# A hybrid encoder on one core: another order for the first transfers, and a warming product between two transposes

## The chip, the core and the metric

The kernel runs on one core of a Trainium2 chip. Its engines are TensorE (PE, matrix products and transposes; its loads of the stationary operand are listed as PEld), VectorE (DVE), ScalarE (ACT), GpSimd (POOL) and SyncE (SP). Each executes its own instructions in order and waits for the others by semaphores. DMA transfers between the chip's memory and the core's working memory are issued by SP, ScalarE and GpSimd, each on a queue of its own, and are carried out by 16 DMA engines. The metric is the device time of one execution in microseconds, as the median of several.

## What is computed

The reference is an encoder of two layers on 256 tokens of 1024 channels, in float32:

```python
def reference(x, w_in, w_pool, ...):
    h = x
    for layer in range(DEPTH):          # 2
        h = h + _token_mixer(_rmsnorm(h, norm1[layer]), w_in[layer], ...)
        h = h + _conv_ffn(_rmsnorm(h, norm2[layer]), w_up[layer], ...)
    return _rmsnorm(h, norm_f)

def _rmsnorm(x, g):
    y = x * lax.rsqrt(jnp.mean(x * x, axis=-1, keepdims=True) + EPS)
    return y * g
```

The token mixer multiplies the normalised x (256 x 1024) by w_in (1024 columns of pooling, 3 x 1536 of queries, keys and values, 2048 of gates), mixes tokens by means over windows and by attention in three groups of heads, and projects back. The second sub-layer is a gated MLP with 2816 channels and a convolution over three tokens. For this document only the very beginning matters: the first norm of x, and the first columns of values, `rmsnorm(x, norm1[0]) @ w_in[0][:, 4096:5120]`.

## The kernel before

All products are made at float32's accuracy out of three products of split operands: a number is kept as a rounded high part and the rest as a low part, and high x high, low x high and high x low are added up in PSUM. For every piece of weights ScalarE rounds the high part and VectorE subtracts the rest (`Weights.open_next`); TensorE then multiplies. Weights come through three raw buffers, which SP loads as soon as a buffer is free.

The beginning is `values_of_x`, written out by hand: its instructions stand on each engine in the order of the program, with no scheduler in between. It makes the first 1024 columns of values for all 256 tokens before x has been normalised. The norm's row norm1[0] scales the rows of the weights, so it must stand as a column, one number for each channel: `gcol`. The norm's other factor, one number per token, comes later, when the sums are copied out. So these are the steps:

- `begin` issues the first transfers. x is held as h with even tokens (t = 0) and odd tokens (t = 1) apart; it comes in parts of 256, 256 and 512 channels for each t (`part_of_x`, L342). The first two megabytes of weights come as `loads[0]` and `loads[1]` in four transfers of 256 KB each (`load_by`, L142), the columns 0 to 511 and 512 to 1023 of the first 512 rows. The norm's row comes as 8 rows of 128 numbers, `rows8`, whose tile is named grows (L349).
- TensorE makes five products of a tile of ones, whose result nobody uses (`warm`, L377, `WARM[0]` = 5, tile gain_ps), transposes rows8 into PSUM (L369), and VectorE copies it to gcol (L370).
- `turn_x` (L719) transposes blocks of x, 128 x 128, into PSUM (xt_ps), since TensorE needs channels on the partitions; ScalarE or VectorE rounds them to xuh (L726), and VectorE leaves the rest in xul (L723). The first call takes two blocks of even tokens, the second two blocks of odd tokens.
- `wait()` makes one more product of ones without a use (`WARM[1]` = 1, tile warm_ps).
- `split(k, g)` rounds piece k of the weights of columns' half g, scaled with gcol, on ScalarE (L199) and makes the rest on VectorE (L200). The tiles of the high and low parts are m, ybig, at (each holds both) or wh and wl.
- `product` (L765, v_ps) multiplies: for each k and g two sets of tokens and three kinds, six products of 128 x 128 with 128 x 512.

Transfers of SP and ScalarE signal on eight semaphores in turn, and the queue of SP waits before it issues a transfer until the one eight before it has landed. GpSimd's transfers have semaphores of their own. From `load_params` on, the rest of the program is ordered by a scheduler.

Of the kernel before, what the change touches and what calls it, by code (L numbers as in the profile page):

```python
# [10 lines left out]
F32 = mybir.dt.float32  # L11
# [5 lines left out]
P = 128  # L17
# [3 lines left out]
KD = D // P  # L21
# [200 lines left out]
def encoder(ctx, tc, x, w_in, w_pool, pool_scale, w_a, w_b, w_o, norm1, norm2, w_up, conv_w,  # L222
            conv_b, w_down, rel_bias, norm_f, onehot, edges, out):
    nc = tc.nc
# [3 lines left out]
    sm = ctx.enter_context(tc.tile_pool(name="small", bufs=2))  # L228
# [7 lines left out]
    def cols(w, c0):  # L236

        src = w[:, c0 : c0 + 256].rearrange("(k p) c -> p k c", p=P)
        return W.add(
            src, (8, 256), [((lambda t, j=j: t[:, :, j * P : (j + 1) * P]), (8, P)) for j in (0, 1)]  # L240
        )

    def rows(w, r0, n=2, c0=0, width=1024, tag=None, pieces=2):

        src = w[r0 : r0 + n * P, c0 : c0 + width].rearrange("(k p) c -> p k c", p=P)
        h = n // pieces
        return W.add(
            src, (n, width), [((lambda t, j=j: t[:, j * h : (j + 1) * h, :]), (h, width)) for j in range(pieces)],
            tag,
        )  # L250

    for l in range(DEPTH):
# [22 lines left out]
        for c in PAIRS:  # L275
            q = cols(w_in[l], C_Q + c * 256)
            k = cols(w_in[l], C_K + c * 256)
# [19 lines left out]
        for kind, n in ORDER.split():  # L297
# [5 lines left out]
            for j in range(2):  # L303
# [14 lines left out]
                else:  # L318
                    p = rows(w_up[l], j * 512, 4, (kind == "g") * DFF + 4 * n * P, 512)
# [4 lines left out]
    h = const.tile([P, 2, D], F32, name="h")  # L324
    xv = x[0].rearrange("(m t) d -> m t d", t=2)
# [11 lines left out]
    def begin():  # L337


        loads = [W.load_by(n) for n in (4, 4, 2, 2)]  # L340

        def part_of_x(t, c, queue=nc.sync):  # L342
            queue.dma_start(out=h[:, t, c], in_=xv[:, t, c])

        first, second, others = slice(0, 256), slice(256, 512), slice(512, D)
        next(loads[0])
        part_of_x(0, first, nc.scalar)
        rows8 = sm.tile([KD, P], F32, tag="gain", bufs=1, name="grows")
        nc.gpsimd.dma_start(out=rows8, in_=norm1[0].rearrange("(k p) -> k p", p=P))  # L349
        part_of_x(1, first)  # L350
        next(loads[1])
        next(loads[0])
        for t in range(2):
            part_of_x(t, second)
        for n in (1, 0, 1):
            next(loads[n])
        for n in range(2):
            part_of_x(n, others)
            next(loads[n])
        for n in (2, 3, 2, 3):  # L360
            next(loads[n])
        ones = sm.tile([P, P], F32, tag="s", name="ones")
        nc.vector.memset(ones, 1.0)
        nc.scalar.copy(out=sm.tile([P, 1], F32, tag="rz", name="table"), in_=ones[:, 0:1])
        make_identity(nc, ident)
        nc.vector.memset(mhalf, -0.5)
        ps = mmp.tile([P, P], F32, tag="mm", name="gain_ps")
        warm(ps, ones, WARM[0])
        nc.tensor.transpose(ps[:, 0:KD], rows8, ident[:KD, :KD])  # L369
        nc.vector.tensor_copy(gcol, ps[:, 0:KD])  # L370
        ps = mmp.tile([P, P], F32, tag="mm", name="warm_ps")
        return lambda: warm(ps, ones, WARM[1])

    def warm(ps, a, n):

        for _ in range(n):
            nc.tensor.matmul(ps, a, a, start=True, stop=True)  # L377
# [324 lines left out]
    def values_of_x(keep_values):  # L702


        wait = begin()
        W.gains = gcol

# [7 lines left out]
        def turn_x(t, c0, n=4):  # L715

            pt = mmp.tile([P, n, P], F32, tag="mm", name="xt_ps")
            for k in range(n):
                nc.tensor.transpose(pt[:, k, :], h[:, t, (c0 + k) * P : (c0 + k + 1) * P], ident)  # L719
            hi, lo = (a[:, c0 : c0 + n, t, :] for a in (xuh, xul))  # L720

            def rest():
                nc.vector.tensor_sub(out=lo, in0=pt, in1=hi.bitcast(F32))  # L723

            def keep(engine=nc.scalar.copy):
                engine(out=hi, in_=pt)  # L726
                return rest

            def copy(f):
                nc.scalar.copy(out=f[:, c0 % 4 : c0 % 4 + n, t, :], in_=pt)  # L730

            return keep, copy
# [17 lines left out]
        def split(k, g):  # L750
            if k % 2 == 0:
                pieces[k, g] = W.n_split
                chunks[k, g], chunks[k + 1, g] = W.open_next()
            hi, lo = chunks[k, g]
            hi()
            return lo
# [29 lines left out]
            return lambda: nc.vector.tensor_sub(out=ol, in0=f, in1=oh.bitcast(F32))  # L786

        fs = [big.tile([P, 4, 2, P], F32, tag=tag, name="xu") for tag in ("q0", "k0")]
        (keep0, copy0), (keep1, copy1) = turn_x(0, 0, 2), turn_x(1, 0, 2)
        wait()  # L790
        rest = keep0(nc.vector.tensor_copy)
        low = split(0, 0)
        rest()
# [86 lines left out]
    for l in range(DEPTH):  # L880
# [21 lines left out]
        if l == 0:  # L902
            with tc.manual_schedule():
                x2 = values_of_x(keep_values)
        else:
            for g in range(2):
                held = begun[0] if g == 0 else [W.get() for _ in range(4)]
                for t in range(2):
                    if g + t == 0:
                        ps = begun[1]  # L910
                    else:
                        ps = v_tile()
                        for n in range(4):
                            v_sum(ps, x2, t, n, held[n])
                    keep_values(t, g, ps)
                for i, _ in held:
                    W.free(i)
# [362 lines left out]
        def first_half():  # L1280
            yield from cross(way[:, 1], way[:, 0])
            for _ in range(2):
                yield
            for t in range(2):
                yield
                keep_merged(0, t, way[:, 1, :, t].rearrange("p i c r -> p c i r"))

        first = first_half()
# [200 lines left out]
```

## Time and profile before

| | |
|---|---|
| time, median of 3 runs | 860.95 us (860.90 to 861.31) |
| time of the profiled execution | 860.72 us |
| its span (first to last instruction) | 858.9 us |
| TensorE busy | 850.1 us, 4036 products |
| VectorE, ScalarE, GpSimd busy | 646.1, 478.7, 19.0 us |
| data moved by DMA | 185.02 MB, 215 GB/s on the mean |

The profile is that of one execution. The 1.8 us between its time and its span lie before the first and behind the last instruction of the program. Times in rows are counted from the start of the span. A row of the timeline gives the start, the length, the engine (with a q for its queue of instructions, where a DMA is issued), the line, the operation with its target and sources, how many there are, and in square brackets how long the engine had idled and what ended it. Products are pipelined, so that the length of one is longer than the distance to the next; the distance is what counts.

### The profile page before, as it was taken

To read this page: it belongs to the slowest core of one execution; us is meant where nothing else is said; L and a number is where in the kernel's file an instruction comes from. 1 tells how busy PE (TensorE), PEld (TensorE's weight loads), DVE (VectorE), ACT (ScalarE), POOL (GpSimd) and SP (SyncE) were. 2 spreads that over 40 slices of the span, in tenths; PEclk is the share of its full clock that TensorE was granted. 3 is DMA by queue.
4 is the path that set the end of the run, shared out by engine and by line. 5 is a ranking of instruction groups with operands and counts; after the bars stand their busy time and mean duration, and the time that the engine had idled before them with its cause. 6 is when DMAs were issued, how large, how long until landed. Compare 5 with 4: busy or idle time off the path is not lost.

```text
span 858.9 us, 11272 instructions
## 1 busy us (share of the span) xinstructions
PE 850.1 (99%) x4036; PEld 714.3 (83%) x4036; DVE 646.1 (75%) x910; ACT 478.7 (56%) x702; POOL 19.0 (2%) x54
## 2 busy tenths in 40 slices
PE   8999999999999999999999999999999999999997
PEld 7888898888888888888888889888888888888885
DVE  4967989566757699999555598886567757998974
ACT  7735475444535576767344446654445436666762
POOL 1120000000010000000000000000000000000001
PEclk9999999999999999999999999999999999999999
DMA  9687585763846777877526776648558376777751
GB/s 316 201 280 248 173 286 157 221 234 123 295 171 212 238 241 242 249 238 270 196 98 201 231 235 206 223 156 247 199 201 285 103 214 211 242 242 240 240 197 50
DMA packets 99628, 185.02 MB, mean 215 GB/s; under 512 B 9630, under 2 KB 26734, under 8 KB 99572
## 3 DMA queue, kind: packets, MB, share of 16 engines
q1 hardware_dynamic: 98900, 182.83, 65.0%
q0 software_dynamic: 528, 1.34, 0.6%
q8 instruction: 32, 0.52, 0.2%
q14 instruction: 24, 0.20, 0.1%
q10 hardware_dynamic: 144, 0.13, 0.0%
HBM read 160.12 MB, written 1.07 MB: 188 GB/s over the span
## 4 chain that ended last, share of the span: by engine, by line
PE 99%; DMA 0%; ACT 0%; issue 0%; POOLq 0%; DVE 0%; POOL 0%; ACTq 0%
PE rows_ps L649 61%; PE res_ps L563 6%; PE res_ps L564 6%; PE res_ps L565 6%; PE v_ps L649 5%; PE proj_ps L535 3%; PE v_ps L765 3%; PE proj_ps L537 2%; PE s_ps L1053 1%; PE o_ps L1128 1%; PE s_ps L1048 1%; PE o_ps L1124 1%; PE xt_ps L496 1%; PE pool_ps L528 0%; PE pool_ps L527 0%; PE pool_ps L529 0%
## 5 line engine op out<-in xcount | busy, mean ns | idle before, releaser
L192 DVE TENSOR_TENSOR wl<-raw,wh 128x1024 fp32r<-128x1024 f32 x278 | 337.0, 1218 | 148.0 <-ACT wh L191 145.6
L649 PE MATMUL rows_ps<-wh,x 128*128 128x512 f32 x1344 | 420.1, 391 | 0.0
L191 ACT CAST wh<-raw 128x1024 fp32r<-128x1024 f32 x278 | 288.9, 1048 | 212.2 <-PE rows_ps L649 129.8
L649 PEld LDWEIGHTS rows_ps<-wh,x 128*128 128x128 f32 x1344 | 252.4, 188 | 52.1
L649 PE MATMUL rows_ps<-wl,x 128*128 128x512 f32 x672 | 261.7, 389 | 0.0
L649 PEld LDWEIGHTS rows_ps<-wl,x 128*128 128x128 f32 x672 | 126.3, 188 | 25.6
L563 PE MATMUL res_ps<-wh,actq 128*128 128x512 f32 (+1 forms) x152 | 57.5, 379 | 0.0
L565 PE MATMUL res_ps<-wh,actk 128*128 128x512 f32 (+1 forms) x152 | 57.5, 378 | 0.0
L564 PE MATMUL res_ps<-wl,actq 128*128 128x512 f32 (+1 forms) x152 | 57.5, 378 | 0.0
L649 PE MATMUL rows_ps<-wh,po 128*128 128x512 f32 x128 | 41.2, 393 | 0.0
L563 PEld LDWEIGHTS res_ps<-wh,actq 128*128 128x128 f32 x152 | 28.6, 188 | 5.4
L565 PEld LDWEIGHTS res_ps<-wh,actk 128*128 128x128 f32 x152 | 28.6, 188 | 5.3
L564 PEld LDWEIGHTS res_ps<-wl,actq 128*128 128x128 f32 x152 | 28.6, 188 | 5.3
L535 PE MATMUL proj_ps<-x,wh 128*128 128x512 f32 x128 | 32.2, 394 | 0.0
L684 DVE STREAM_TRANSPOSE up_rows<-rows_ps 128x512 f32<-128x512 f32 x40 | 26.3, 693 | 3.1 <-PE rows_ps L649 3.1
L649 PEld LDWEIGHTS rows_ps<-wh,po 128*128 128x128 f32 x128 | 24.1, 188 | 4.9
L462 ACT ACTIVATE junk<-h 128x512 f32<-128x512 f32 (+1 forms) x20 | 10.9, 547 | 30.8 <-DVE h L460 30.8
L1356 ACT ACTIVATE yg<-a,prm 128x256 f32<-128x256 f32 x44 | 26.5, 602 | 1.5
L563 PE MATMUL res_ps<-wh,m 128*128 128x512 f32 (+1 forms) x72 | 26.9, 374 | 0.0
L535 PEld LDWEIGHTS proj_ps<-x,wh 128*128 128x128 f32 x128 | 23.1, 189 | 4.2
L565 PE MATMUL res_ps<-wh,m 128*128 128x512 f32 (+1 forms) x72 | 26.4, 367 | 0.0
L564 PE MATMUL res_ps<-wl,m 128*128 128x512 f32 (+1 forms) x72 | 26.4, 366 | 0.0
(214 smaller groups left out, 1051.0 us busy)
## 6 DMA issues: line engine op xcount, KB each, us to landing
raw<-in_w_in_dram SPq DMA_DIRECT2D x56, 1024.0 KB, 5.3
raw<-in_w_up_dram SPq DMA_DIRECT2D x40, 1024.0 KB, 6.3
raw<-in_w_down_dram SPq DMA_DIRECT2D x22, 1024.0 KB, 5.1
up_turned<-up_rows SPq DMA_DIRECT2D x160, 64.0 KB, 3.9
raw<-in_w_a_dram SPq DMA_DIRECT2D x8, 1024.0 KB, 5.4
raw<-in_w_o_dram SPq DMA_DIRECT2D x8, 1024.0 KB, 6.9
qk<-qk_rows SPq DMA_DIRECT2D x64, 64.0 KB, 2.1
pt<-rows SPq DMA_DIRECT2D x64, 64.0 KB, 3.7
```

What stands on the lines that cost most here:

```text
L191: lambda: nc.scalar.copy(out=h, in_=src),
L192: lambda: nc.vector.tensor_sub(out=l, in0=src, in1=h.bitcast(F32)),
L462: nc.scalar.activation(junk[:, 0 : cc.stop - cc.start], h[:, t, cc], AF.Square, scale=D**-0.5, accum_out=ss[:, n : n + 1],)
L535: nc.tensor.matmul(ps, wh(k), x2[:, k], start=(k == 0), stop=False)
L537: nc.tensor.matmul(ps[:, 1], wl(k), x2[:, k, 0], start=False, stop=(k == nk - 1))
L563: nc.tensor.matmul(ps, ah, wh, start=first, stop=False)
L564: nc.tensor.matmul(ps, ah, wl, start=False, stop=False)
L565: nc.tensor.matmul(ps, al, wh, start=False, stop=last)
L649: nc.tensor.matmul(ps, x2[:, 2 * n + j, part, t, :], w[:, j, :], start=(n + m == 0), stop=(n == of - 1 and m == 5),)
L684: nc.vector.transpose(out=out[:, :, t].rearrange("p j c r -> p c j r"), in_=ps[t].rearrange("p (c j r) -> p c j r", c=4, j=4),)
L765: return nc.tensor.matmul(ps[g][t], a[:, k, t, :], w[:, k % 2, :], start=k == 0 and kind == "hh", stop=k == KD - 1 and kind == "hl",)
L1356: nc.scalar.activation(y, aj, AF.Identity, bias=b, scale=w1)
```

## The change

The transfer of the norm's row moves from GpSimd's queue to ScalarE's, where it is the only one. x's even tokens (first 256 channels) move from ScalarE's queue to the head of SP's, ahead of the first weights. The product without a use, `wait()`, is issued between the transposes of even and of odd tokens, where it stood behind both.

```diff
-        def part_of_x(t, c, queue=nc.sync):
-            queue.dma_start(out=h[:, t, c], in_=xv[:, t, c])
+        def part_of_x(t, c):
+            nc.sync.dma_start(out=h[:, t, c], in_=xv[:, t, c])
 
         first, second, others = slice(0, 256), slice(256, 512), slice(512, D)
+        rows8 = sm.tile([KD, P], F32, tag="gain", bufs=1, name="grows")
+        nc.scalar.dma_start(out=rows8, in_=norm1[0].rearrange("(k p) -> k p", p=P))
+        part_of_x(0, first)
         next(loads[0])
-        part_of_x(0, first, nc.scalar)
-        rows8 = sm.tile([KD, P], F32, tag="gain", bufs=1, name="grows")
-        nc.gpsimd.dma_start(out=rows8, in_=norm1[0].rearrange("(k p) -> k p", p=P))
         part_of_x(1, first)
         next(loads[1])
         next(loads[0])
...
-        (keep0, copy0), (keep1, copy1) = turn_x(0, 0, 2), turn_x(1, 0, 2)
+        keep0, copy0 = turn_x(0, 0, 2)
         wait()
+        keep1, copy1 = turn_x(1, 0, 2)
```

On TensorE, at the program's start, the rows of before (-) and now (+) are these; gain_ps<-ident,grows is the transpose of the norm's row, warm_ps the product without a use, and the names in brackets are the semaphores waited for (DMAHW of the queues of SP and ScalarE, DMASW of GpSimd's):

```order
-L369 MATMUL gain_ps<-ident,grows 128x8 [waits DMASW0_49,Pool_49]
-L719 MATMUL xt_ps<-ident,h 128x128 [waits DMAHW0_49]
-L719 MATMUL xt_ps<-ident,h 128x128
-L719 MATMUL xt_ps<-ident,h 128x128 [waits DMAHW2_49]
+L369 MATMUL gain_ps<-ident,grows 128x8 [waits DMAHW0_49,Pool_49]
+L719 MATMUL xt_ps<-ident,h 128x128 [waits DMAHW1_49]
 L719 MATMUL xt_ps<-ident,h 128x128
 L377 MATMUL warm_ps<-ones 128x128
+L719 MATMUL xt_ps<-ident,h 128x128 [waits DMAHW3_49]
+L719 MATMUL xt_ps<-ident,h 128x128
 L765 MATMUL v_ps<-m_151,xuh 128x512 [waits DVE_49,Activation_49]
```

The warming product has moved ahead of the transposes that wait for x's odd tokens; from the first v_ps on, TensorE's order is the old one.

On SP's queue, the start of the program now reads (raw_91 and raw_94 are the first and the second weights, h is x):

```order
L343 DMA h<-in_x_dram 128x256
L142 DMA raw_91<-in_w_in_dram 128x512
L343 DMA h<-in_x_dram 128x256
L142 DMA raw_94<-in_w_in_dram 128x512
L142 DMA raw_91<-in_w_in_dram 128x512
L343 DMA h<-in_x_dram 128x256 x2
L142 DMA raw_94<-in_w_in_dram 128x512 [waits DMAHW0_49]
L142 DMA raw_91<-in_w_in_dram 128x512 [waits DMAHW1_49]
```

The first row is new here and every other stands one place later; the transfer in the last row but one did not wait before and now waits for the norm's row (DMAHW0). Behind this, the engines' orders and waits are those of before, with the semaphores' numbers shifted by one.

## The prediction

> **What bounds the kernel now.** I read the page first: the busy times and the chain that ended last.
>
> ```profile
> span 858.9 us, 11272 instructions
> ...
> PE 850.1 (99%) x4036; PEld 714.3 (83%) x4036; DVE 646.1 (75%) x910; ACT 478.7 (56%) x702; POOL 19.0 (2%) x54
> ...
> PE 99%; DMA 0%; ACT 0%; issue 0%; POOLq 0%; DVE 0%; POOL 0%; ACTq 0%
> ```
>
> TensorE works for 850.1 of 858.9 us and is 99% of the chain: the kernel ends when its matmuls end. So time can be won only where TensorE idles, or where a matmul takes longer than it need. The chain's first 25 us say where it idles (start, length, what):
>
> ```profile
> 1.27 3.60 DMA grows<-in_norm_dram
> 4.87 0.14 issue
> 5.01 0.24 PE gain_ps L369
> 5.25 1.04 PE xt_ps L719 x4
> 6.30 0.43 PE warm_ps L377 x2
> 6.72 4.53 PE v_ps L765 x12
> ```
>
> The chain starts with the transfer of the first norm's row, 3.60 us from POOL's issue to landing at 4.87. Its transpose into a column comes next on TensorE, then four transposes of x, a product without a use, and the real products. Next, TensorE in four stretches (length; busy us and instructions; granted clock; DMA share; GB/s), and single products on either side of 10.4 us:
>
> ```profile
> 1.04:3.54 2.50, 2.50 (x10) 1.00 0.65 140
> 3.54:4.98 1.44, 0.00 (x1) 1.00 1.09 384
> 4.98:10.40 5.42, 5.39 (x17) 1.00 0.99 320
> 10.40:17.00 6.60, 6.60 (x32) 1.00 1.03 391
> ```
>
> ```profile
> 6.48 0.76 PE L765 MATMUL v_ps<-m,xuh 128*128 128x512 f32 x1
> ...
> 9.18 0.63 PE L765 MATMUL v_ps<-wh,xuh 128*128 128x512 f32 x1
> 9.60 0.63 PE L765 MATMUL v_ps<-wh,xul 128*128 128x512 f32 x1
> ...
> 13.38 0.39 PE L765 MATMUL v_ps<-wl,xuh 128*128 128x512 f32 x1
> 13.61 0.39 PE L765 MATMUL v_ps<-wh,xuh 128*128 128x512 f32 x1
> ...
> 14.29 0.39 PE L765 MATMUL v_ps<-m,xuh 128*128 128x512 f32 x1
> ```
>
> There are two losses. TensorE idles 1.44 us (3.54 to 4.98) between the warming products and the norm row's transpose. And up to about 10.4 us it runs at half speed: the same product follows the one before it after 0.42 us (9.18, 9.60), later after 0.23 (13.38, 13.61). The granted clock reads 1.00 in every stretch, so the view's clock column does not show this; the durations do. Nine real products lie between 6.48 and 10.40, 3.92 us for what would take 9 x 0.23 = 2.07: 1.85 us lost. The speed did not rise after 2.50 us of work from 1.04 on, and it did after 5.39 us of work from 4.98 on.
>
> [...]
>
> **The change, part by part.** Who issues what first:
>
> ```profile
> 0.72 0.41 ACTq L343 DMA_DIRECT2D h<-in_x_dram  x1
> 0.73 0.39 SPq L142 DMA_DIRECT2D raw<-in_w_in_dram  x1
> 1.17 0.42 SPq L343 DMA_DIRECT2D h<-in_x_dram  x1
> 1.27 0.75 POOL L349 DMA_DIRECT2D grows<-in_norm_dram  x1 [0.84 <-POOLq L1471]
> ...
> 3.53 1.84 SPq L142 DMA_DIRECT2D raw<-in_w_in_dram  x3
> ```
>
> And from issue to landing (last column, us): the weights' transfer that was issued at 1.64 beside the norm's row, and the shortest of the page's groups:
>
> ```profile
> raw<-in_w_in_dram SPq DMA_DIRECT2D x1, 256.0 KB, 3.7
> grows<-in_norm_dram POOLq DMA_DIRECT2D x1, 4.0 KB, 3.6
> ```
>
> ```profile
> qk<-qk_rows SPq DMA_DIRECT2D x64, 64.0 KB, 2.1
> ```
>
> 1. The norm's row leaves POOL (issue at 1.27) for ScalarE's queue (slot at 0.72), alone there. No row shows so small a transfer on that queue. Bounds: 3.7 us as the weights took, so 4.4; and 2.1 as the 64 KB of the page's group took later in the program, so 2.8. I take 3.3, nearer the lower end: 4 KB ahead of any backlog, where POOL's was issued 0.55 later behind 512 KB of others. TensorE's warming ends at 3.54, so up to there the landing costs nothing. POOL loses a DMA issue of 0.75 us and makes the identity that much earlier; it was not late. ScalarE issues one DMA as before, 0.41.
>
> 2. SP now issues x's even tokens at 0.73, the first weights at about 1.17, x's odd tokens at about 1.6; everything behind is one slot later, 0.44 us as from 0.73 to 1.17. The bytes ahead of each are the same as before or fewer for x, and the transfers run near their rate (384 GB/s in the idle stretch), so the slots should hardly show. Before, all three were in by 4.98, as no transpose waited. By the 3.7 us of the weights' row, the first weights were in at 0.73 + 3.7 = 4.43, and the same 512 KB now end no later; x's even part, 128 KB and first in line, comes well before that. The bad end is that the first weights land 0.44 later, at 4.87.
>
> 3. SP's eighth transfer, the second weights' second quarter, now waits for the norm row's semaphore, the one eight transfers earlier. SP's seventh came up at 3.53, so the eighth comes at about 4.0, and a landing at 3.3 costs nothing; at 4.4 it would cost SP 0.4 us, with all later loads behind it.
>
> 4. The product without a use moves between the two pairs of transposes, at no extra work. It fills the time in which x's odd part is still on its way.
>
> First product: TensorE's own work from the norm's transpose on is 6.48 - 5.01 = 1.47 us, so 3.54 + 1.47 = 5.0 if nothing is waited for. ScalarE's first split took 0.72:
>
> ```profile
> 5.49 0.72 ACT L199 ACTIVATE m<-raw,gcol 128x512 fp32r<-128x512 f32 x1 [2.84 <-DVE gcol L370]
> ```
>
> From weights at 4.43 it ends at 5.15 and the product follows at 5.25; from weights at 4.87, at 5.7. I take 5.3, between 5.0 and 5.7. Gain at the start: 6.48 - 5.3 = 1.2.
>
> The clock: the idle stretch of 1.44 us closes to some tenths at most, so TensorE works without a pause from 1.04. With the 5.4 us that the trace shows, products are fast from 6.4 instead of 10.4. Then (6.4 - 5.3) / 0.43 = 2.6 products are slow, 2.6 x 0.2 = 0.5 us lost instead of 1.85: gain 1.3. Together 2.5 us.
>
> What is late next: the splits. The rows of ScalarE and VectorE behind it:
>
> ```profile
> 8.47 0.72 ACT L199 ACTIVATE wh<-raw,gcol 128x512 fp32r<-128x512 f32 x1
> ...
> 11.51 0.37 ACT L726 CAST xuh<-xt_ps 128x256 fp32r<-128x256 f32 x1 [1.09 <-PE xt_ps L719]
> ...
> 17.65 0.59 ACT L726 CAST xuh<-xt_ps 128x512 fp32r<-128x512 f32 x1 [0.83 <-PE xt_ps L719]
> ```
>
> ```profile
> 12.81 0.75 DVE L200 SCALAR_TENSOR_TENSOR m<-raw,gcol,m 128x512 fp32r<-128x512 f32 x1 [0.20 <-ACT m L199]
> ```
>
> The split at 8.47 needs SP's eighth transfer. The transfers are near their rate (320 GB/s to 10.40) and no byte ahead of it is gone, so I leave it where it is. Behind it ScalarE's order is fixed and had 1.09 us of idle time before 11.51; only that can close. VectorE's rest of the weights, done at 13.56, is used by the third product of the group that begins at 14.29, so at 14.75: 1.19 us in hand. 1.09 + 1.19 = 2.3 us is the most that TensorE can come earlier at that place without stalling; with the eighth transfer 0.44 later, 1.85. So 2.5 is cut to 2.0, between 1.85 and 2.3. At 17.65 ScalarE waited another 0.83 us for TensorE, so there the room is larger, and all later work is in its old order: the gain stays.
>
> Sum against the profiled execution: 860.72 - 2.0 = 858.7. It is 0.23 below the median of 860.95; I go by the median: 859.0.
>
> **The rivals.** *Transposes do not count as work for the clock.* Then the moved product stands alone between transposes, and the speed rises only after an unbroken row of products. Before, that took from 6.48 to 10.40, 3.92 us; the same from 5.3 on gives 9.2, so everything shifts by the 1.2 of the start alone: 859.8. For it: the rise came 3.9 us after the first product. Against: it came 5.4 us after the transposes as well, and one trace cannot part them. [...]
>
> *The speed rises at a fixed time, 10.4, whatever is done before.* The 1.2 us then hold 1.2 / 0.43 = 2.8 slow products, worth 2.8 x 0.23 = 0.65 us: 860.3. Against: the two busy stretches above fit a count of work.
>
> *Slower.* All splits need the norm's column, all transposes stand behind it on TensorE's queue, and the eighth transfer of SP waits for its row. Should the row be starved on ScalarE's ring by SP's transfers, the start is its landing plus 1.6 (4.87 to 6.48). It decides from a landing at 4.87 on; over 1.7 us worse from about 6.6, 5.9 us after its issue: 862.7 or more. Against: the longer of the early transfers above took 3.7 us.
>
> *Nothing*: x's odd part or the weights come as late as the old first product needed them (weights by 5.49): within 0.3 of 860.95.
>
> **How the numbers follow.** Early clock 0.55 (2.0 won, own range 1.7 to 2.5), start only 0.28 (1.2), fixed time 0.08 (0.65), nothing 0.04, slower 0.05. 0.2% of 861 us, about what a measurement of this kernel tells from no change, is 1.72 us. Nearly all of the first case lies beyond it, the next three do not: faster 0.54, same 0.41, slower 0.05. The range reaches from 2.5 won (858.4) to 0.5 won (860.45), which leaves out the end of the third case and the last two.
>
> **What would show it.** In the profile after, TensorE has no idle stretch over 0.4 us between 1.04 and the first product, that product starts near 5.3, products 0.23 apart begin near 6.4, and before 8, and the group that began at 14.29 begins near 12.2. The forecast is wrong if the norm's row lands after 3.6, if products stay 0.42 apart to 9 us though TensorE did not pause, or if TensorE pauses for the split at 8.47.

## The result, and the profile after

The changed kernel takes 859.15 us (median of 20 runs, 858.83 to 859.76). The kernel before, run 20 times in turn with it, takes 860.53 us (859.56 to 861.34). The ratio is 0.9983, with a 95% interval from 0.9977 to 0.9990: 1.4 us are won, 0.17%. The runs also lie closer together, 0.9 us from end to end instead of 1.8.

The profiled execution took 859.12 us, 1.6 less than that of before. From the page after:

```profile
span 857.3 us, 11270 instructions
...
PE 849.8 (99%) x4036; PEld 712.5 (83%) x4036; DVE 646.0 (75%) x910; ACT 478.2 (56%) x702; POOL 18.4 (2%) x53
```

TensorE's busy time has hardly changed, 849.8 for 850.1 us: by the page, 1.3 of the 1.6 us are idle time that has gone. This number hides short waits, though: a fast product counts as busy for 0.39 us and the next one follows after 0.23, so a wait of up to 0.16 us behind each product counts as busy too. The four stretches of TensorE after (length; busy us and instructions; granted clock; DMA share; GB/s):

```profile
1.04:3.54 2.50, 2.50 (x11) 1.00 0.56 160
3.54:4.98 1.44, 1.44 (x9) 1.00 0.98 331
4.98:10.40 5.42, 5.37 (x23) 1.00 0.97 321
10.40:17.00 6.60, 6.41 (x33) 1.00 1.05 397
```

The idle stretch from 3.54 to 4.98 is full, and from 4.98 to 10.40 there are 23 instructions instead of 17, since the products are faster. But two small losses are new: 5.37 of 5.42 and 6.41 of 6.60. TensorE's timeline after shows the places:

```profile
3.48 0.27 PE L369 MATMUL gain_ps<-ident,grows 8*128 8x8 f32 x1
3.68 0.69 PE L719 MATMUL xt_ps<-ident,h 128*128 128x128 f32 x2
4.16 0.63 PE L377 MATMUL warm_ps<-ones 128*128 128x128 f32 x2
4.59 0.64 PE L719 MATMUL xt_ps<-ident,h 128*128 128x128 f32 x2
4.98 0.54 PE L765 MATMUL v_ps<-m,xuh 128*128 128x512 f32 x1
...
6.57 0.39 PE L765 MATMUL v_ps<-m,xul 128*128 128x512 f32 x1
6.80 0.40 PE L765 MATMUL v_ps<-wh,xuh 128*128 128x512 f32 x1
...
8.83 0.40 PE L765 MATMUL v_ps<-m,xul 128*128 128x512 f32 x1
9.28 0.72 PE L765 MATMUL v_ps<-m,xuh 128*128 128x512 f32 x2
...
11.67 0.40 PE L765 MATMUL v_ps<-wl,xuh 128*128 128x512 f32 x1
12.22 0.51 PE L765 MATMUL v_ps<-m,xuh 128*128 128x512 f32 x1
12.56 0.40 PE L765 MATMUL v_ps<-m,xul 128*128 128x512 f32 x1
13.00 0.74 PE L765 MATMUL v_ps<-m,xuh 128*128 128x512 f32 x2
```

The first product begins at 4.98 instead of 6.48. From 6.57 on most products are 0.23 apart instead of 0.43. The trace also records the moment at which the granted clock goes to full speed: 10.33 before and 5.12 now. Then there are longer distances: 0.45 from 8.83 to 9.28, 0.55 from 11.67 to 12.22, 0.44 from 12.56 to 13.00. The group that began at 14.29 begins at 12.22, 2.1 earlier, but its third product only at 13.00 for 14.74, 1.7 earlier. This is what reaches the end (the table behind the experiments shows it for other kernels too). ScalarE's timeline after tells why:

```profile
4.18 0.72 ACT L199 ACTIVATE m<-raw,gcol 128x512 fp32r<-128x512 f32 x1 [1.35 <-DMA raw<-in_w_in_dram]
...
7.71 0.73 ACT L199 ACTIVATE m<-raw,gcol 128x512 fp32r<-128x512 f32 x1 [0.98 <-DMA raw<-in_w_in_dram]
...
9.06 0.72 ACT L199 ACTIVATE wh<-raw,gcol 128x512 fp32r<-128x512 f32 x1 [0.37 <-DMA raw<-in_w_in_dram]
```

Three splits now wait for weights; before, none did by the profile. And the chain of the work that ended last, which before was TensorE alone from 5.01 on, runs through a transfer of weights, ScalarE and VectorE up to 13.00:

```profile
4.48 5.20 DMA raw<-in_w_in_dram
...
9.69 1.32 ACT junk L737 x4
11.02 0.26 ACT xuh L726
11.27 0.27 ACT xu L730
11.54 0.63 ACT m L199
12.17 0.02 issue
12.20 0.76 DVE m L200
12.96 0.04 issue
13.00 2.57 PE v_ps L765 x10
```

The two squares of x's first half (junk, 1.32 us) stand in it, between the split at 9.06 and the next turn of x. The view lets them follow a transfer that landed at 9.69. They read x and not weights, though, and ScalarE was in the split from 9.06 until then: what held them was that split, which had itself waited for its weights.

### The profile page after: what moved, and what is told of

Its sections match the earlier page's. It is cut to its first block, busy times and chain, and to the rows that moved or that the text cites. A ratio compares the mean times of both kernels' runs of the same rounds, so it can differ in the third digit from the quotient of the medians.

```text
span 857.3 us, 11270 instructions
## 1 busy us (share of the span) xinstructions
PE 849.8 (99%) x4036; PEld 712.5 (83%) x4036; DVE 646.0 (75%) x910; ACT 478.2 (56%) x702; POOL 18.4 (2%) x53
## 4 chain that ended last, share of the span: by engine, by line
PE 98%; DMA 1%; ACT 0%; SPq 0%; DVE 0%; issue 0%; POOLq 0%; POOL 0%; ACTq 0%
PE rows_ps L649 61%; PE res_ps L565 6%; PE res_ps L563 6%; PE res_ps L564 6%; PE v_ps L649 5%; PE proj_ps L535 3%; PE v_ps L765 2%; PE proj_ps L537 2%; PE s_ps L1054 1%; PE o_ps L1129 1%; PE s_ps L1049 1%; PE o_ps L1125 1%; PE xt_ps L496 1%; DMA raw<-in_w_in_dram 1%; PE pool_ps L529 0%; PE pool_ps L528 0%
```

## The experiments

The theory: the speed of products rises after TensorE has worked without a pause for long enough (in the trace of before not after 2.50 us, but after 5.39), the old pause of 1.44 us hindered that, and after the change the second weights' splits and ScalarE's order behind them set the pace. The rivals: the start alone; the moved product; transposes that do not count. Each experiment was run in turn with the kernel before, 10 or 11 runs beside 32 or 33 of before, whose medians were 860.24 us (beside the transfers alone, the moved product alone, the three more warming products and the kernel without warming), 860.54 (the row alone, the odd part, the squares later and both) and 860.50 (the other four).

**The transfers alone**, the moved product back behind both pairs:

```diff
-        keep0, copy0 = turn_x(0, 0, 2)
+        (keep0, copy0), (keep1, copy1) = turn_x(0, 0, 2), turn_x(1, 0, 2)
         wait()
-        keep1, copy1 = turn_x(1, 0, 2)
```

> The new order of transfers alone; the product without a use stays behind both pairs of transposes. Theory (early row, work without a pause, then the second weights set the pace): x's odd part landed at 4.5 in the changed kernel, the even transposes end near 4.2, so a pause of 0.3 us appears, the first product is near 5.0 as in the changed kernel, products are fast by 8 at the latest, and the time is 859.2 (859.0 to 859.5). Rival (the moved product is what keeps the clock's count going): the rise comes 2 to 3 us later and the time is 859.7 to 860.2.

859.00 us (858.47 to 859.84), ratio 0.9985 (0.9976 to 0.9993): the whole gain. The first product is at 4.98, as with the moved product. x's odd tokens come so early that the four transposes follow each other:

```profile
3.68 1.21 PE L719 MATMUL xt_ps<-ident,h 128*128 128x128 f32 x4
4.73 0.39 PE L377 MATMUL warm_ps<-ones 128*128 128x128 f32 x2
4.98 0.47 PE L765 MATMUL v_ps<-m,xuh 128*128 128x512 f32 x1
```

**The moved product alone**, on the old transfers:

```diff
-        (keep0, copy0), (keep1, copy1) = turn_x(0, 0, 2), turn_x(1, 0, 2)
+        keep0, copy0 = turn_x(0, 0, 2)
         wait()
+        keep1, copy1 = turn_x(1, 0, 2)
```

> The old order of transfers; only the product without a use moves between the transposes. Theory: the pause of 1.4 us before the norm row's transpose stays, the first product stays near 6.5, 860.5 (860.2 to 860.8). Rival (the moved product has a part of its own in the gain): 859.9 or less.

860.80 us, ratio 1.0002 (0.9993 to 1.0011): no change. Of the two edits only the transfers have an effect.

**The old transfers with the pause filled by three more warming products**:

```diff
-WARM = (5, 1)
+WARM = (8, 1)
```

> The kernel before with eight products without a use instead of five, so that TensorE works from 1.04 to about 5.0 and the pause is filled, with no transfer moved. Theory (work without a pause sets the clock): the first product is near 6.3, products are fast by then or soon after instead of near 10, 1.0 to 1.7 us are won: 859.1 (858.8 to 859.6), with a smaller spread of the times than before. Rival (the gain is the earlier start alone): 860.5 or, for the later row's transpose, 860.6.

859.28 us (859.12 to 859.44), ratio 0.9986 (0.9977 to 0.9994): the same gain within the intervals, though no transfer has moved and the first product is as late as before. The runs lie 0.3 us apart, where those of before in the same batch lie 1.9 apart. TensorE's timeline of this kernel:

```profile
1.04 3.79 PE L377 MATMUL gain_ps<-ones 128*128 128x128 f32 x16 [1.04 <-DVE mhalf L366]
4.97 0.24 PE L369 MATMUL gain_ps<-ident,grows 8*128 8x8 f32 x1
...
6.44 0.58 PE L765 MATMUL v_ps<-m,xuh 128*128 128x512 f32 x1
...
8.03 0.40 PE L765 MATMUL v_ps<-m,xul 128*128 128x512 f32 x1
8.26 0.39 PE L765 MATMUL v_ps<-wh,xuh 128*128 128x512 f32 x1
```

Products are 0.23 apart at 8.03 instead of 0.43 up to 10, and the trace records full speed from 6.67 on, for 10.33 before. So the clock alone is worth 1.2 us by the ratio and 1.0 by the medians, and "the start alone" falls.

**The pause filled with transposes** of the tile of ones instead, six, with a result that nobody uses:

```diff
         warm(ps, ones, WARM[0])
+        for _ in range(6):
+            nc.tensor.transpose(ps, ones, ident)
```

> The kernel before, its transfers untouched, with six transposes of the tile of ones behind the five warming products (about 0.24 us each, from 3.54 to about 5.0), whose result nobody uses. If transposes count as work for the clock, this is the kernel with eight warming products again: 859.3 (859.1 to 859.6), products fast by 8.4, all runs close together. If they do not count, it is the kernel before: 860.2 to 860.8 with runs spread from 859.6 to 861.4, products fast between 8.4 and 11.9.

859.24 us (858.86 to 859.47), ratio 0.9986 (0.9977 to 0.9994). Full speed is recorded from 6.28 on, for 6.67 with the products in the pause and 10.33 before:

```profile
1.04 2.50 PE L379 MATMUL gain_ps<-ones 128*128 128x128 f32 x10 [1.04 <-DVE mhalf L366]
3.34 1.49 PE L370 MATMUL gain_ps<-ident,ones 128*128 128x128 f32 x6
...
7.93 0.40 PE L767 MATMUL v_ps<-m,xul 128*128 128x512 f32 x1
8.17 0.40 PE L767 MATMUL v_ps<-wh,xuh 128*128 128x512 f32 x1
```

**The changed kernel without any warming product**, all six left out; by the theory the rise comes later then:

```diff
-WARM = (5, 1)
+WARM = (0, 0)
```

> The changed kernel with no product without a use at all (six are left out, no result depends on them). [...] Rival (the clock has no part, the start alone): 859.15. Rival (the speed rises at a fixed time): as the changed kernel, 859.15.

859.45 us, ratio 0.9991 (0.9983 to 1.0000), the runs from 859.09 to 861.12. The median is 0.3 us above the 859.15 of both rivals: six of the eleven runs lie between 859.09 and 859.45, five between 859.89 and 861.12. With no warming, the profiled run was slow for long (full speed at 10.49, for 5.12 in the changed kernel's):

```profile
2.29 0.24 PE L369 MATMUL gain_ps<-ident,grows 8*128 8x8 f32 x1 [2.29 <-DMA grows<-in_norm_dram]
3.20 0.69 PE L719 MATMUL xt_ps<-ident,h 128*128 128x128 f32 x2 [0.67 <-DMA h<-in_x_dram]
4.46 0.69 PE L719 MATMUL xt_ps<-ident,h 128*128 128x128 f32 x2 [0.57 <-DMA h<-in_x_dram]
4.94 0.80 PE L765 MATMUL v_ps<-m,xuh 128*128 128x512 f32 x1
...
9.37 0.63 PE L765 MATMUL v_ps<-wh,xul 128*128 128x512 f32 x1
9.80 0.63 PE L765 MATMUL v_ps<-wl,xuh 128*128 128x512 f32 x1
```

Its span is 858.1 us, 0.8 more than with warming. Twelve slow products at 0.2 would have cost 2.4: the larger part falls into time in which the changed kernel waits for its splits. These rows also show by when the first transfers, whose order is that of the changed kernel, had landed, which the warming hides: the norm's row at 2.29, x's even tokens at 3.2, the odd ones at 4.46.

**The norm's row alone on the other queue**, SP's order as before, x's even part on ScalarE's queue behind the row:

```diff
+        rows8 = sm.tile([KD, P], F32, tag="gain", bufs=1, name="grows")
+        nc.scalar.dma_start(out=rows8, in_=norm1[0].rearrange("(k p) -> k p", p=P))
         next(loads[0])
         part_of_x(0, first, nc.scalar)
-        rows8 = sm.tile([KD, P], F32, tag="gain", bufs=1, name="grows")
-        nc.gpsimd.dma_start(out=rows8, in_=norm1[0].rearrange("(k p) -> k p", p=P))
```

> The old order on SP; only the norm's row moves to ScalarE's queue, and x's even part stays on that queue, behind it. Theory: the row lands near 3.3 as in the changed kernel, x's even part is issued 0.6 us later than before and lands at 4.7 to 5.0, TensorE pauses about 1.1 us for it, the first product is near 6.2 and the clock rises about as late as before; the second weights land as before (7.1 and 8.45): 860.2 (859.8 to 860.5). Rival (the row alone is what counts): 859.15.

859.35 us, ratio 0.9985 (0.9976 to 0.9993): the whole gain, against the expectation. The pause for x was 0.51, half of what was expected, the first product at 5.56, and the profiled run fast from 8.2. In this run full speed came at 8.07, 3 us later than in the changed kernel's profile, and the two times are alike (859.28 and 859.12): what the changed kernel gains by its earlier start and clock it loses again in waits for the splits. Two splits wait here too, though SP's order of loads is that of before:

```profile
7.38 0.72 ACT L199 ACTIVATE m<-raw,gcol 128x512 fp32r<-128x512 f32 x1 [0.52 <-DMA raw<-in_w_in_dram]
...
8.74 0.72 ACT L199 ACTIVATE wh<-raw,gcol 128x512 fp32r<-128x512 f32 x1 [0.38 <-DMA raw<-in_w_in_dram]
```

The row's queue is the part of the change that matters.

**x's odd part on ScalarE's queue** behind the row, so that SP has one transfer fewer to issue ahead of the later loads:

```diff
-        part_of_x(1, first)
+        part_of_x(1, first, nc.scalar)
         next(loads[1])
```

> The changed kernel with x's odd part on ScalarE's queue behind the row, so that everything behind it on SP is one slot (0.47 us) earlier. Theory (the slots on SP set when the second weights land, and these set the pace from 7 to 13 us): the split that waited until 7.71 and the one at 9.06 come 0.3 to 0.5 us earlier, and so does everything behind: 858.8 (858.6 to 859.0). Rival (the bytes set it): the splits stay, 859.15.

859.89 us, ratio 0.9990 (0.9981 to 0.9999), but in two groups: three runs from 858.24 to 858.74, eight from 859.70 to 860.63. The splits of the second weights did come earlier, at 6.73 and 7.78 in the profiled run (858.24) for 7.71 and 9.06. This one was the fastest of the eleven, with full speed from 5.08 on, although its first product is at 5.62, later than in the changed kernel. But TensorE now pauses 0.30 us for the odd tokens; that the clock rises late in the eight slower runs is read from their times alone.

**The changed kernel with the squares later**, behind the next two pieces' splits on ScalarE:

```diff
-        for t in range(2):
-            square(t, 0)
         for t, (keep, copy) in enumerate(turns):
             rest = keep()
             copy(fs[0])
             rest()
             both(2, t)
+        for t in range(2):
+            square(t, 0)
```

> The changed kernel with ScalarE's two squares of x's first half (9.69 to 10.92) behind the next two pieces' splits instead of ahead of them. Theory (ScalarE's chain behind the second weights sets the pace at the group that begins at 12.22): the pauses of TensorE between 11.9 and 13.0 go, 0.5 to 0.9 us are won there, and up to 0.4 are lost again where the later splits come behind the squares: 858.7 (858.4 to 859.1). Rival (the weights' landing alone sets it, the squares stand in its shadow): 859.15 or more.

858.34 us (858.19 to 859.31), ratio 0.9975 (0.9966 to 0.9985): 0.8 us less than the changed kernel by the medians. TensorE has no gap left after 4.98, although in this profiled run the speed rose late, at 7.48, and the split still came at 9.01:

```profile
4.98:10.40 5.42, 5.42 (x22) 1.00 0.94 317
10.40:17.00 6.60, 6.60 (x36) 1.00 1.05 406
```

So ScalarE's order behind that split held the rest of the gain, not the weights' landing alone. The median shows it better than this profile, in which the later clock by itself closes some gaps.

**Both**, x's odd part on ScalarE's queue and the squares later.

> Both of the last two edits together. Theory: what they win adds up, less what later splits give back: 858.3 (858.0 to 858.8). Rival: one of them takes away what the other would win, 858.8 or more.

859.65 us, ratio 0.9984 (0.9975 to 0.9992), from 857.93 to 860.18: again two groups. The profiled runs of the last and of the one with the odd part alone make a pair. Both pause before the odd tokens' transposes, 0.30 and 0.29 us, at the same moment. With the odd part alone:

```profile
5.10 0.44 PE L719 MATMUL xt_ps<-ident,h 128*128 128x128 f32 x2 [0.30 <-DMA h<-in_x_dram]
5.62 0.50 PE L765 MATMUL v_ps<-m,xuh 128*128 128x512 f32 x1
5.96 0.39 PE L765 MATMUL v_ps<-m,xul 128*128 128x512 f32 x1
```

With both:

```profile
5.08 0.69 PE L719 MATMUL xt_ps<-ident,h 128*128 128x128 f32 x2 [0.29 <-DMA h<-in_x_dram]
5.59 0.79 PE L765 MATMUL v_ps<-m,xuh 128*128 128x512 f32 x1
6.18 0.63 PE L765 MATMUL v_ps<-m,xul 128*128 128x512 f32 x1
```

The first is already fast at its transposes (0.44 for two), the second is slow until 10; the clocks' records say 5.08 and 10.10. One kernel's work up to there is the other's, so what differs is not the work; what it is, no run shows. The changed kernel and the one with the squares later make another such pair, without a pause: the same instructions up to 9.69, and full speed from 5.12 in one profile and from 7.48 in the other.

**The two last with one more product between the transposes**, so that the pause is filled:

```diff
-WARM = (5, 1)
+WARM = (5, 2)
```

> The kernel with x's odd part on ScalarE's queue, with two products without a use between the transposes instead of one, so that TensorE's pause of 0.5 us before the odd tokens' transposes (4.6 to 5.1) is filled. Theory (a pause of half a microsecond starts the clock's count again): the runs, which lay between 858.2 and 860.6, draw together at their low end, 858.4 (858.2 to 858.7). Rival (x's odd part on the other queue costs that time itself): as before the edit, a median of 859.5 or more with the same spread.

> The same with ScalarE's two squares behind the next two pieces' splits. Theory: the runs, which lay between 857.9 and 860.2, draw together at their low end, 858.0 (857.8 to 858.4), the fastest of all. Rival: no faster than the changed kernel with the squares later alone, 858.3 or more.

With the odd part alone: 858.59 us, ratio 0.9981 (0.9972 to 0.9990); nine of eleven runs lie between 858.17 and 858.82, two still at 860.1 and 860.2. Before it was three of eleven. With the squares later too: 858.39 us (858.09 to 858.90), ratio 0.9977 (0.9968 to 0.9986), and no run stays behind. So with the pause of 0.3 us eight and six of eleven runs lie in the slower group, and with it filled two of eleven and none of ten: by the times, it put off the rise in most runs here. A pause of this length does not always do so, as the next experiment shows. That version is as fast as the simpler one with the squares alone (858.34); the two cannot be told apart.

**The old transfers with eight warming products and the squares later**:

> The kernel before with eight warming products and the squares later, no transfer moved. Theory (with the clock up early, splits and not the first product's start set the pace up to 13 us): with the second weights 0.5 us earlier than in the changed kernel this comes as far as the changed kernel with the squares later, 858.4 (858.2 to 858.8). Rival (the earlier start of 1.5 us counts once the splits let TensorE run): 859.0 or more.

859.21 us, ratio 0.9987 (0.9978 to 0.9995): nothing more than eight warming products alone (859.28). Here the first product was at 6.68. TensorE paused for 0.38 us in the profiled run, from 4.83 to 5.21; behind that the stretches show no gap (5.19 us busy of the 5.42 from 4.98 to 10.40, 0.23 of it the pause, and all of the 6.60 to 17.00), and yet full speed came at 6.33 and all eleven runs lie within 0.6 us. What makes a short pause matter stays open. Against 858.34 for the changed kernel with the squares later, the early transfers are worth 0.9 us once ScalarE's order lets TensorE run. The theory's expectation falls; the rival, that the start then counts, holds.

**The profiled executions side by side.** The table gives the start of the first product, the moment of full speed by the trace's record of the clock, how many products began before it, the start of the third product of the group that begins at 14.29 in the kernel before, and the time, all in us.

| kernel | first product | full speed | slow products | that third product | time |
|---|---|---|---|---|---|
| before | 6.48 | 10.33 | 9 | 14.74 | 860.72 |
| changed | 4.98 | 5.12 | 1 | 13.00 | 859.12 |
| eight warming products | 6.44 | 6.67 | 1 | 13.29 | 859.27 |
| changed, no warming | 4.94 | 10.49 | 12 | 14.01 | 860.01 |
| row alone | 5.56 | 8.07 | 6 | 13.25 | 859.28 |
| odd part on ScalarE's queue | 5.62 | 5.08 | 0 | 12.26 | 858.24 |
| squares later | 4.97 | 7.48 | 6 | 12.66 | 858.52 |

In all fourteen profiled executions the time is 845.9 to 846.1 us more than the start of that third product, whatever the kernel: the first 13 us decide, and all that is won there reaches the end. Neither the first product nor the clock decides alone.

## Why the prediction was right, and where it was not

The forecast of 859.0 met 859.15 and its mechanism is the one found: an earlier start and an earlier clock, cut by the splits behind them. That the number is so close is in part luck, as the base hides a miss: 2.0 us were to be won on 860.95, the median of three runs of before, and 1.4 were won on 860.53, the median of twenty. The runs of before scatter by 1.8 us and three of them were too few. Against the profiled executions, the gain is 1.6.

1. *The norm's row lands at 3.3, between 2.8 and 4.4.* It had landed by 2.3 in the kernel without warming, 1.6 us after its issue, below the lower bound. The 64 KB transfers of later stages (2.1 us) were no lower bound for these 4 KB on an empty queue. It cost nothing, as forecast, since the warming products end at 3.54.
2. *The first weights come at 4.43 and the first product at 5.3.* They came by 4.18 and it began at 4.98: 1.5 us won at the start, for 1.2.
3. *SP's eighth transfer does not wait for the row.* Right: it was issued at 4.0.
4. *The moved product fills the wait for x's odd tokens.* There was hardly a wait to fill; alone it did nothing, and without it the time was the same.
5. *Products are fast from 6.4.* In the profiled execution full speed came at 5.12, 4.1 us after TensorE's work began, and one product was slow instead of 2.6. With the squares later it came at 7.48 after the same work, and six were slow. So the 5.4 us that one trace had shown are no fixed count; 6.4 lies between what two executions show. The limit of 8 for the rise was the author's estimate, which no trace of before shows; both of these lie below it. The clock's share was put at 1.3; the kernel with the pause filled and no transfer moved won 1.2 by the ratio, 1.0 by the medians. The loss of 1.85 in the kernel before was 0.2 too high: nine fast products took 2.3 us (5.62 to 7.90 with the odd part on ScalarE's queue) and not 9 x 0.23, since some wait for their inputs.
6. *The cut from 2.5 to 2.0 by the splits.* Right in its place, too small in its size, and this is the term that failed. The split at 8.47 was left there, with 0.44 later as the bad end. It came at 9.06, 0.59 later, and the split ahead of it waited too (0.98), which the sum had not. 2.3 less 0.59 is 1.7, and that is what the third product of the group at 12.22 shows. An estimate of the cut from the table: the start won 1.5, eight slow products less at 0.2 each won 1.6, and 1.7 of these 3.1 reached the third product, so that 1.4 was lost where the sum had 0.5. "No byte ahead of it is gone" was true, but SP issues one transfer after the other, and the x part that had gone out beside SP's on ScalarE's queue now takes a slot ahead of the weights (3.53 became 4.01). With x's odd part moved to ScalarE's queue the two splits began 1.0 and 1.3 us earlier. That the slot alone makes them late is not shown: these gains are more than one slot, and with the row alone on ScalarE's queue the splits waited until 7.38 and 8.74, though SP's order was that of before.

So the likeliest case held in its mechanism, while its own range, 1.7 to 2.5 won, was too high at 1.4 by the medians: the chance of 0.54 for more than 0.2% rested on the term that was mis-sized. *Transposes do not count* falls: six of them filled the pause as well as products did (859.24 and 859.28, full speed at 6.28 and 6.67). *A fixed time* falls: in the profiled runs full speed came between 4.31 and 10.49. *Slower* did not occur; the row was not starved.

What stays open is how much of the spread of before's 1.8 us is the clock's: it shrinks to 0.3 us when the pause is filled, but the moment of the rise was seen only in profiled runs. Open too is why a pause of 0.3 us put the rise off in some runs of one kernel, while one of 0.38 us did not in another, and what besides the slot on SP delays the second weights.

## What to carry to other kernels

Where TensorE bounds a kernel, look at its first ten microseconds for pauses while the first data come: filling a pause of 1.4 us with products, or transposes, that nobody uses was worth nearly as much here (1.2 us by the ratio) as the whole new order of transfers (1.4). An earlier start pays only as far as the next producer allows (by the estimate above, 1.7 us of 3.1 here); follow the splits or copies behind it and see which transfer each waits for and what stands between them on that engine. The transfer moved to the head of SP's queue took a slot from the next seven there, 0.45 to 0.48 us (0.73 became 1.18, 3.53 became 4.01), though the bytes were the same; the one behind these, which had waited until 4.57, was issued at 4.48.

## What the runs showed of the hardware

A transfer of 4 KB on ScalarE's otherwise empty queue was there 1.6 us after its issue (0.72 to 2.29, in the kernel without warming); through GpSimd's queue, issued 0.55 us later behind 512 KB of others, it took 3.6. Two kernels with the same work at first and the same pause of 0.3 us on TensorE reached full speed at 5.08 and at 10.10; eight of eleven runs of the first lie in its slower group, and two of eleven with the pause filled. Without any pause, two with the same work at first reached it at 5.12 and 7.48. With six float32 transposes through the identity in the pause full speed came at 6.28, with three more products at 6.67, with neither at 10.33, in one profiled execution each; both versions with the pause filled took 0.9986 of the time of before. The granted clock in the stretches' view read 1.00 all the while; the distances between products (0.43 and then 0.23 us) showed it, and the trace's record of the clock, which begins with full speed (10.33 before, 5.12 after).
